# The end of mixer B in a two-layer encoder on one Trainium2 core: row sums through DRAM, and the order and buffers of the last p products

## The chip, the core and the metric

The kernel runs on one core of one Trainium2 chip. TensorE (PE) multiplies and transposes 128x128 blocks into PSUM. VectorE (DVE), ScalarE (ACT) and GpSimd (POOL) do the elementwise work, and SyncE (SP) issues most of the DMAs; its queue is served in order. Each engine runs its own list of instructions in the order in which the program issues them, and waits for the others by semaphores. The metric is the device time of one execution in microseconds; the runs before are given by their median.

## What is computed

The reference is an encoder trunk over 1024 tokens of width 1024, in float32, with two layers. Cut to what matters here:

```python
for i in range(DEPTH):                     # 2 layers
    h = rms_norm(x, norm_g[i])
    if i % 2 == 0:
        y = mixer_a(h, ...)                # neighbourhood attention, 16 heads of 64
    else:
        y = mixer_b(h, ...)                # grouped-query attention, 16 q heads, 4 kv heads
    x = x + y                              # y = (attention * silu(gate)) @ w_out
    g = sigmoid(rms_norm(x, ple_norm_g[i]) @ ple_w_gate[i])
    x = x + g * (p[i] @ ple_w_proj[i])
return rms_norm(x, final_norm_g)
```

Both mixers end their attention with a softmax: the products with v have to be divided by the row sums of the exponentials and multiplied with the gate before the output projection.

## The kernel before

To keep float32 accuracy every matmul is done as three: each operand is split into a high half (`...h`) and a low half (`...l`), and high x high, high x low and low x high are added in PSUM (`split3`, L321). ACT makes the high halves by a copy, DVE the low ones by a subtraction. Weights pass through `wstage` and are split by `WQ.pump` (L215: ACT at L228, DVE at L233), one call of which stands in each pulse.

The program has four stages: mixer A (layer 0), `dense_phase(0)` (output projection in Strassen form, `strassen_out`, and the gated embedding), mixer B (layer 1), `dense_phase(1)`. Each mixer walks through 16 heads, in pairs. In mixer B a step n of 128 is one head, one half `hf` of the tokens and one block of 128 queries t. For each step PE forms scores (`f_S`, L1246, into the pool "s"), DVE their minimum (L1256), ACT the exponential with the row sum in `rs` (`f_E`), PE transposes the result P (`f_T`, L1272, into the pool "t"), ACT and DVE copy it to PTh and PTl (L1274, L1275), and every second step PE multiplies with v (`f_AV`, L1280, into the pool "o", which has one buffer).

The dense products are spread between these pieces by `mix` (L366): a list `att` of attention pieces with costs, a list `dense` of products with costs, and a product is issued as soon as its share of the costs lags behind that of the attention. After each attention piece comes a `pulse` (L345): one `WQ.pump`, and one tick of `post`, a list of closures with a number of ticks to wait. `later` is a second such list; mixer B ticks it once a step, and what is left at the end of a mixer is flushed. In the last quarter of mixer B (g == 3, steps 96 to 127) the dense list holds 16 gate products and the 16 products of p with its projection (`pp_items`), here called p products. A p product is six matmuls into a buffer of the pool "d" (one buffer in mixer B), a copy by ACT to `th` (L629) and a store to DRAM (L630, `ppD`). The last three of the list are held back (`hold`): `mix` issues one of them ahead of the last transposes, where nothing else stands between two sets of transposes (kind "apart"), and two at the very end.

`head_end` (L494) is called by both mixers after the last product with v of a head and a half. ACT copies the lower half of "o" to Y (`evac`, L542), DVE adds the upper half (`join`, L506), which frees "o", and takes the reciprocals of the row sums (`norm`, L532). The sums lie one query to a partition, and are needed one query to a column, in all partitions, in the buffer rb. For pairs 0 to 6 (`rows`, L508) DVE turns a 32x32 block (L510), and SP stores the rows to DRAM (four DMAs, L513) and loads them back spread over the partitions (two DMAs, L515). For pair 7, in both halves, DVE spreads the sums over rb (`spread`, L519), and PE turns them by four transposes (`across`, L525) into PSUM: a buffer of "o" in mixer B, of "t" in mixer A. For the first half ACT copies the result to rb (L528); for the second DVE reads it from PSUM. `DT` holds the ticks after which `across` is issued, five and two. `fin_last` (L554) is the end of pair 7: Y times the gate G (L555), Y times the turned sums (L559), and the high and low halves (L564, L567) into HTh and HTl, which the output projection reads.

The next stage begins with the products of the Strassen form: four blocks with b11, four with b21, four with t2 and so on. Beside the first eight DVE forms the sums S (L1427 to L1435), and it splits the weight t2 (L1401).

Of the kernel before, what the change touches and what calls it, by code (L numbers as in the profile page):

```python
# [11 lines left out]
F32 = mybir.dt.float32  # L12
# [3 lines left out]
AF = mybir.ActivationFunctionType  # L16
# [15 lines left out]
CB = (1.25, 1.0, 2.0, 0.5, 1.0)  # L32
# [2 lines left out]
KT, KN = 2, 4  # L35
DO = (2, 3)
DD = ((3, 2), (3, 2))
DT = (5, 2)
FIN = (4, 4)
HOLD = 2  # L40
ENTRY = 8
# [119 lines left out]
def trunk(ctx, tc, x, wts, rpb, gains, hgains, mask, sides, rope, gain0, out):  # L161
    nc = tc.nc
    sync, act, dve, pool, pe = nc.sync, nc.scalar, nc.vector, nc.gpsimd, nc.tensor
# [152 lines left out]
    post = Later()  # L316
# [28 lines left out]
    def pulse():  # L345
        WQ.pump()
        post.tick()
# [18 lines left out]
    def mix(att, dense, lead=0, hold=0):  # L366
        for f, _ in dense[:lead]:
            f()
            pulse()
        kept = dense[len(dense) - hold:]  # L370
        dense = list(dense[lead:len(dense) - hold])
        total = sum(c for _, c in dense)
        span = sum(c for _, c in att)
        spent = done = 0.0
        since = True
        for i, (f, c) in enumerate(att):
            kind = getattr(f, "kind", None)
            if kind == "apart" and not since and (dense or len(kept) > 2):
                d, e = (dense or kept).pop(0)
                d()  # L380
                spent += e
            if kind in ("apart", "blocks"):
                since = False
            f()
            leave.run()
            pulse()
            done += c
            while dense and spent < total * done / span - 1e-6:
                leave.run()
                leave.wait = i + 1 < len(att) and getattr(att[i + 1][0], "first", False)  # L390
                d, c = dense.pop(0)
                d()
                leave.wait = False
                spent += c
                since = True
        leave.run()
        for f, _ in dense + kept:
            f()
            pulse()
# [94 lines left out]
    def head_end(sb, h, hf, rs, Ops, ylive, layer, gg, talloc):  # L494
        pair = h // 2
        b = (h % 2) * 64
        if h % 2 == 0:
            Y = sb.tile([128, 512], F32, name="Y", bufs=3 if layer == 0 else 2)
            rb = sb.tile([128, 512], F32, name="rb", bufs=2)
            r8 = sb.tile([128, 8], F32, name="r8", bufs=4)  # L500
            ylive[pair, hf] = (Y, rb, r8, {})
        Y, rb, r8, tail = ylive[pair, hf]
        yh = Y[b:b + 64]

        def join():
            dve.scalar_tensor_tensor(yh, Ops[0:64], 0.5, yh, op0=ALU.mult, op1=ALU.add)  # L506

        def rows():  # L508
            r8T = sb.tile([128, 32], F32, name="r8T", bufs=2)
            dve.transpose(r8T.rearrange("p (a c) -> p a c", a=4), r8[:, None].to_broadcast([128, 4, 8]))  # L510
            rD = dram.tile([8, 128], F32, name="rD", bufs=4)
            for b in range(4):
                post.add(DD[layer][1], lambda b=b: sync.dma_start(rD[:, 32 * b:32 * b + 32], r8T[32 * b:32 * b + 8]))  # L513
            for i in range(2):
                post.add(DD[layer][1], lambda i=i: sync.dma_start(  # L515
                    rb[64 * i:64 * i + 64], bass.AP(tensor=rD.tensor, offset=rD.offset + 512 * i, ap=[[0, 64], [1, 512]])))

        def spread():
            dve.tensor_copy(rb.rearrange("p (t j c) -> p t j c", t=4, j=2),  # L519
                            r8.rearrange("p (j t) -> p t j", j=2)[:, :, :, None].to_broadcast([128, 4, 2, 64]))  # L520

        def across():
            ps = talloc()
            for t in range(4):
                pe.transpose(ps[:, t], rb[:, t * 128:(t + 1) * 128], ident)  # L525
            ps = ps.rearrange("p t c -> p (t c)")
            if hf == 0:
                act.activation(rb, ps, AF.Copy)  # L528
            tail["rb"] = rb if hf == 0 else ps

        def norm():
            dve.reciprocal(r8[:, 4 * (h % 2):4 * (h % 2) + 4], rs)  # L532
            if h % 2 == 0:
                return
            if pair < 7:
                post.add(DD[layer][0], rows)
            else:
                spread()
                post.add(DT[hf], across)

        def evac():
            act.activation(yh, Ops[64:128], AF.Copy, scale=0.5)  # L542
            post.add(DY, join)
            norm()
        if h == NH - 1 and hf == 1:
            evac()
        else:
            post.add(DO[layer], evac)
        if h % 2 == 0:
            return None  # L550
        G = gg.pop((pair, hf))
        del ylive[pair, hf]

        def fin_last():  # L554
            dve.tensor_tensor(Y, Y, G, ALU.mult)  # L555
            if "rb" not in tail:
                post.l = [e for e in post.l if e[1] is not across]
                across()
            dve.tensor_tensor(Y, Y, tail["rb"], ALU.mult)  # L559
            y3 = Y.rearrange("p (t c) -> p t c", t=4)  # L560
            ts = slice(4 * hf, 4 * hf + 4)

            def hi():
                act.activation(HTh[:, ts, 7, :], y3, AF.Copy)  # L564

            def lo():
                dve.tensor_tensor(HTl[:, ts, 7, :], y3, HTh[:, ts, 7, :], ALU.subtract)  # L567
            if hf == 0:
                post.add(3, hi)
                post.add(5, lo)  # L570
            else:
                hi()
                lo()

        def fin():
            yhi, ylo = rb.bitcast(F32R), Y.bitcast(F32R)

            def store(c, src):
                sync.dma_start(yD[layer][c][4 * hf:4 * hf + 4, :, pair, :].rearrange("t p c -> p t c"),
                               src.rearrange("p (t c) -> p t c", t=4))  # L580

            def split():
                act.activation(yhi, Y, AF.Copy)
                dve.tensor_tensor(ylo, Y, yhi, ALU.subtract)
                post.add(2, lambda: (store(0, rb), store(1, Y)))
            pool.tensor_tensor(Y, Y, G, ALU.mult)
            pool.tensor_tensor(Y, Y, rb, ALU.mult)
            if pair < 4 and hf == 1:
                post.add(YS[layer] + 2, lambda: store(0, Y))
            else:  # L590
                post.add(YS[layer], split)
        return fin_last if pair == 7 else fin
# [452 lines left out]
    def mixer_b(pend):  # L1045
        with ExitStack() as es:
# [5 lines left out]
            psS = es.enter_context(tc.tile_pool(name="bps", bufs=2, space=PSUM))  # L1052
# [7 lines left out]
            def dalloc():  # L1060
                if pro[0]:
                    pro[1] += 1
                    if pro[1] <= ENTRY:
                        return psS.tile([128, 1024], F32, name="s")[:, :512]
                    if pro[1] % 2 == 0:
                        return psO.tile([128, 512], F32, name="o")
                return pd.tile([128, 512], F32, name="d")

            gg, ylive = {}, {}
            KA, KB, V, QT, QST, P, RS, OP = {}, {}, {}, {}, {}, {}, {}, {}  # L1070
            later = Later()
# [172 lines left out]
            steps = [(2 * p + j, hf, t) for p in range(8) for hf in range(2) for j in range(2) for t in range(4)]  # L1244
# [35 lines left out]
            def f_AV(h, hf, t):  # L1280
                if t == 1:
                    OP[h, hf] = psO.tile([128, 512], F32, name="o")
                o = OP[h, hf][:, (t - 1) * 128:(t + 1) * 128]
                for k in range(NT):
                    mm(o, V[h // 4][:, k], PTh[:, k], t == 1 and k == 0, False)
                while turned:
                    turned.pop(0)()
                for k in range(NT):
                    mm(o, V[h // 4][:, k], PTl[:, k], False, t == 3 and k == NT - 1)
                if t == 3:  # L1290
                    fin = head_end(sb, h, hf, RS[h, hf], OP.pop((h, hf)), ylive, 1, gg, talloc)
                    if fin:
                        later.add(FIN[1], fin)
# [29 lines left out]
            for g in range(4):  # L1323
                att = []
# [26 lines left out]
                    if YLOAD_B <= n < YLOAD_B + NT:  # L1351
                        att.append((lambda t=n - YLOAD_B: load_y(1, t), 0.0))
                if g == 3:
                    att.append((lambda: f_AV(*steps[-1]), CB[1]))
                def gates(p):
                    return [i for hf in range(2) for i in gate_items("bg", p, hf, dalloc, sb, gg)]
                dense = []
# [7 lines left out]
                else:  # L1365
                    WQ.cap[3] = 2
                    dense += gates(2 * g + 1) + pp_items(1, dalloc, sb, TAGS_B)
                mix(att, dense, hold=HOLD + 1 if g == 3 else 0)
            post.flush()
            later.flush()  # L1370
            post.flush()
# [453 lines left out]
```

## Time and profile before

| what | us |
|---|---|
| median of 3 runs | 1514.3 |
| lowest and highest run | 1509.89, 1514.97 |
| the profiled execution | 1510.65 |
| its span, first to last instruction | 1508.9 |
| PE busy | 1483.4 |
| DVE busy | 1088.7 |
| ACT busy | 917.7 |

A row of a timeline in the following reads: start in us from the start of the span, duration in us, engine, line of the kernel, operation, output <- inputs by the program's names, shapes, and a count where several instructions are merged (the duration is then that of them all); in brackets stands how long the engine was idle before it, and what ended that. PE's matmuls are pipelined, so the next one starts before the end that is shown of the last: distances of starts say more than durations. A row of the list of waits reads: engine, what and line that waited, what it waited for, us in total, times, longest. PEld is the load of weights into PE, SPq the DMAs that SP issues.

### The profile page before, as it was taken

The numbers are of one execution on the slowest core, as the hardware profiler recorded it, in microseconds if no ns is written. First come the engines' busy times: TensorE is split into PE (matmuls) and PEld (weight loads), VectorE is DVE, ScalarE is ACT, GpSimd is POOL, SyncE is SP. The second block draws the span as 40 slices with busy tenths as digits, with TensorE's granted clock in tenths as the row PEclk, the third lists the DMA queues.
The fourth block names the chain that finished last, engine by engine and source line by source line (L and its number), as shares of the span: only waits on it lengthen the run. The fifth ranks groups of instructions, "written<-read, shape, count | busy, mean of one in ns | idle before, by whom it ended". The sixth has DMA issues, their size and how long they took to land.

```text
span 1508.9 us, 24794 instructions
## 1 busy us (share of the span) xinstructions
PE 1483.4 (98%) x8885; PEld 1304.4 (86%) x8885; DVE 1088.7 (72%) x2139; ACT 917.7 (61%) x1866; POOL 449.3 (30%) x605
## 2 busy tenths in 40 slices
PE   9999999999999999999999999999999999999997
PEld 8888988988988787888988989989999988888786
DVE  7566476477477498767887786777877887689856
ACT  7676476476477535433567776766767777744432
POOL 1456475386265200010322222443131300000022
PEclk9999999999999999999999999999999999999999
DMA  8334374283132862262210111111111122763123
GB/s 266 123 104 123 79 170 137 64 172 95 36 92 82 324 246 99 91 206 80 76 50 22 33 53 39 43 33 46 55 30 46 39 76 78 230 240 116 56 91 133
DMA packets 91243, 157.45 MB, mean 104 GB/s; under 512 B 18160, under 2 KB 54256, under 8 KB 90608
## 3 DMA queue, kind: packets, MB, share of 16 engines
q1 hardware_dynamic: 85968, 139.86, 28.2%
q0 software_dynamic: 2560, 8.39, 3.7%
q10 hardware_dynamic: 2592, 7.61, 1.5%
q8 instruction: 71, 1.16, 0.3%
q14 instruction: 52, 0.43, 0.1%
HBM read 125.30 MB, written 50.83 MB: 117 GB/s over the span
## 4 chain that ended last, share of the span: by engine, by line
PE 44%; DVE 6%; ACT 2%; issue 1%; POOL 0%; ACTq 0%; DVEq 0%; POOLq 0%
PE d L319 19%; PE o L319 9%; PE s L319 8%; PE t L1272 7%; PE t L319 1%; DVE xn L1607 1%; DVE PTl L1275 1%; DVE X L1503 0%; DVE mn L1256 0%; PE t L1226 0%; DVE HTl L492 0%; DVE HTl L1449 0%; PE t L490 0%; DVE wl L233 0%; DVE th L1665 0%
## 5 line engine op out<-in xcount | busy, mean ns | idle before, releaser
L319 PE MATMUL d<-wh,HTh 128*128 128x256 f32 (+1 forms) x1000 | 332.2, 335 | 0.9 <-DVE X L1503 0.6
L319 PE MATMUL d<-wh,HTl 128*128 128x256 f32 (+1 forms) x1000 | 327.5, 330 | 0.0
L319 PE MATMUL d<-wl,HTh 128*128 128x256 f32 (+1 forms) x1000 | 326.8, 330 | 0.2 <-DVE wl L1401 0.2
L1275 DVE TENSOR_TENSOR PTl<-t,PTh 128x512 fp32r<-128x512 f32 x256 | 164.6, 685 | 106.3 <-ACT PTh L1274 106.0
L319 PEld LDWEIGHTS d<-wh,HTh 128*128 128x128 f32 x1000 | 188.1, 190 | 20.9 <-issue 1.0
L319 PEld LDWEIGHTS d<-wl,HTh 128*128 128x128 f32 x1000 | 188.1, 189 | 19.9 <-DVE wl L1401 0.6
L319 PE MATMUL d<-HTh,wh 128*128 128x512 f32 x504 | 204.7, 406 | 0.0
L319 PEld LDWEIGHTS d<-wh,HTl 128*128 128x128 f32 x1000 | 188.0, 189 | 18.3
L319 PE MATMUL d<-HTh,wl 128*128 128x512 f32 x504 | 198.0, 393 | 0.0
L319 PE MATMUL d<-HTl,wh 128*128 128x512 f32 x504 | 197.4, 392 | 0.0
L1262 ACT ACTIVATE P<-s,mn 128x1024 f32<-128x1024 f32 x128 | 142.9, 1116 | 47.3 <-DVE mn L1256 46.4
L1274 ACT ACTIVATE PTh<-t 128x512 fp32r<-128x512 f32 x256 | 139.4, 595 | 46.0 <-PE t L1272 45.5
L1256 DVE TENSOR_REDUCE mn<-s 128x1 f32<-128x1024 f32 x128 | 155.1, 1211 | 9.8 <-PE s L319 9.3
L798 POOL TENSOR_TENSOR PTh<-PTh,SIDE 128x256 fp32r<-128x256 f32 x96 | 81.2, 846 | 195.4 <-ACT PTh L793 195.4
L1272 PE MATMUL t<-ident,P 128*128 128x128 f32 x1024 | 134.9, 273 | 2.5 <-DVE PTl L1275 2.0
L319 PE MATMUL s<-KA,QS 128*128 128x512 f32 (+2 forms) x384 | 134.2, 403 | 0.3 <-DVE mn L772 0.3
L1272 PEld LDWEIGHTS t<-ident,P 128*128 128x128 f32 x1024 | 115.5, 140 | 12.8 <-DVE PTl L1275 6.9
L319 PE MATMUL s<-KB,QS 128*128 128x512 f32 (+2 forms) x384 | 121.5, 370 | 0.0
L319 PE MATMUL o<-PTl,V 128*128 128x256 f32 (+2 forms) x672 | 120.0, 290 | 1.1 <-DVE PTl L1275 0.6
L319 PE MATMUL o<-PTh,V 128*128 128x256 f32 (+2 forms) x672 | 118.4, 287 | 1.9 <-DVE Y L506 0.8
L233 DVE TENSOR_TENSOR wl<-wstage,wh 128x1024 fp32r<-128x1024 f32 x78 | 98.0, 1258 | 29.8 <-ACT wh L228 29.3
L319 PEld LDWEIGHTS d<-HTh,wl 128*128 128x128 f32 x504 | 94.6, 188 | 21.7
(250 smaller groups left out, 2891.2 us busy)
## 6 DMA issues: line engine op xcount, KB each, us to landing
wstage<-in_wts SPq DMA_DIRECT2D x88, 512.0 KB
pp<-ppD SPq DMA_DIRECT2D x32, 256.0 KB
X<-in_x SPq DMA_DIRECT2D x15, 512.0 KB
rb<-rD SPq DMA_DIRECT2D x56, 128.0 KB
ppD<-th SPq DMA_DIRECT2D x20, 256.0 KB
tD0t<-in_wts SPq DMA_DIRECT2D x16, 256.0 KB
tD1t<-in_wts SPq DMA_DIRECT2D x16, 256.0 KB
xD<-X SPq DMA_DIRECT2D x8, 512.0 KB
```

The lines of the kernel that those rows point to most:

```text
L233: eng.tensor_tensor(lo[:, c:c + n], s[:, c:c + n], hi[:, c:c + n], ALU.subtract)
L319: pe.matmul(ps, a, b, start=first, stop=last, skip_group_check=True)
L798: pool.tensor_tensor(pt[:, 3 * j - 1:3 * j + 4:4], pt[:, f1:f1 + 1].to_broadcast([128, 2, 128]), SIDE[:, :2], ALU.mult)
L1256: dve.tensor_reduce(mn, ps, axis=AX.X, op=ALU.min)
L1262: act.activation(p, ps, AF.Exp, bias=mn, scale=-1.0, accum_out=RS[h, hf][:, t:t + 1])
L1272: pe.transpose(ps[:, i], p[:, k * 128:(k + 1) * 128], ident)
L1274: act.activation(PTh[:, ks, c], ps, AF.Copy)
L1275: dve.tensor_tensor(PTl[:, ks, c], ps, PTh[:, ks, c], ALU.subtract)
L1607: dve.scalar_tensor_tensor(xn, X[t], rn[m][:, i:i + 1], g1, op0=ALU.mult, op1=ALU.mult)
```

## The change

Four edits. In `norm` the first half of pair 7 takes the way of the other pairs: `rows`, through DRAM, with rb ready for `fin_last` by its dependencies alone; the copy out of PSUM in `across` is gone, and `DT` is one number. In `mix` a piece of kind "last" is preceded by a kept product and a pulse. The last products with v in mixer B become such a piece, and four products are kept instead of three, so that one goes ahead of the last transposes, one ahead of the last products with v, and two behind. From that piece on `dalloc` takes turns: the next buffer from the pool "s", the one after from "d".

```diff
-DT = (5, 2)
+DT = 2
...
-            if kind == "apart" and not since and (dense or len(kept) > 2):
+            if kind == "apart" and not since and (dense or len(kept) > 3):
...
+            if kind == "last" and kept:
+                kept.pop(0)[0]()
+                pulse()
             f()
...
-            ps = ps.rearrange("p t c -> p (t c)")
-            if hf == 0:
-                act.activation(rb, ps, AF.Copy)
-            tail["rb"] = rb if hf == 0 else ps
+            tail["rb"] = ps.rearrange("p t c -> p (t c)")
...
-            if pair < 7:
+            if pair < 7 or hf == 0:
                 post.add(DD[layer][0], rows)
+                tail["rb"] = rb
             else:
                 spread()
-                post.add(DT[hf], across)
+                post.add(DT, across)
...
+                if end[0]:
+                    end[0] += 1
+                    if end[0] % 2 == 0:
+                        return psS.tile([128, 1024], F32, name="s")[:, :512]
                 return pd.tile([128, 512], F32, name="d")
...
-                    att.append((lambda: f_AV(*steps[-1]), CB[1]))
+                    def last():
+                        end[0] = 1
+                        f_AV(*steps[-1])
+                    last.kind = "last"
+                    att.append((last, CB[1]))
...
-                mix(att, dense, hold=HOLD + 1 if g == 3 else 0)
+                mix(att, dense, hold=HOLD + 2 if g == 3 else 0)
```

More of the change, by code (lines that the diff above doesn't have):

```diff
@@ L1066, in dalloc @@
                         return psO.tile([128, 512], F32, name="o")
+                if end[0]:
+                    end[0] += 1
+                    if end[0] % 2 == 0:
+                        return psS.tile([128, 1024], F32, name="s")[:, :512]
                 return pd.tile([128, 512], F32, name="d")
+            end = [0]
             gg, ylive = {}, {}
```

## The prediction

> **What bounds the kernel now.** I read the page first, then the list of waits for TensorE over the last quarter of mixer B, then timelines around the two places where rows of sums are turned, then the rows of the DMA queue.
>
> ```profile
> span 1508.9 us, 24794 instructions
> PE   1483.4 (98%) x8885; PEld 1304.4 (86%) x8885; DVE 1088.7 (72%) x2139; ACT 917.7 (61%) x1866; POOL 449.3 (30%) x605
> ```
>
> PE is at 98%: the time is PE's work plus its few waits, so only PE instructions that go and PE waits that go or come count. In the last quarter of mixer B (1184 to 1326 us) the waits are these, with three more in rows below:
>
> ```profile
> PE t L1272 <- DVE PTl L1275: 0.9, 1, 0.9
> PE o L319 <- DVE Y L506: 0.8, 2, 0.5
> ...
> PE o L319 <- ACT PTh L1274: 0.4, 1, 0.4
> ```
>
> There is little to win: some 4 us of waits in 142 us. The diff, however, touches the shared `head_end`, so `pair < 7 or hf == 0` also changes the end of mixer A, which the change's few words leave out. Both ends have to be summed.
>
> **Mixer B, the four transposes that go.** Between the transposes of P and the next scores lie 0.79 us in an ordinary step (1289.17 to 1289.96), and 2.29 us in the step with the transposes of the row sums (1292.36 to 1294.65):
>
> ```profile
> 1289.17 1.04 PE L1272 MATMUL t<-ident,P 128*128 128x128 f32 x8
> ...
> 1289.96 0.71 PE L319 MATMUL s<-KA,QS 128*128 128x512 f32 x2
> ...
> 1292.36 1.03 PE L1272 MATMUL t<-ident,P 128*128 128x128 f32 x8
> ...
> 1294.24 0.66 PE L525 MATMUL o<-ident,rb 128*128 128x128 f32 x4 [0.84 <-DVE Y L506]
> 1294.65 0.71 PE L319 MATMUL s<-KA,QS 128*128 128x512 f32 x2
> ...
> 1306.79 0.69 DVE L559 TENSOR_TENSOR Y<-Y,rb 128x512 f32<-128x512 f32 x1
> ```
>
> The difference, 1.5 us, is the four transposes and their wait for the join of Y, which frees the one o buffer. It goes: **-1.5 us**. ACT also loses the copy of the turned rows. DVE loses a copy and gains a 32x32 transpose, which took 0.20 us for another pair (row below) and lies beside PE's work.
>
> The price is the trip through DRAM: four stores and two loads on SP's queue, the loads waiting there for the stores. Two trips of other pairs bound it, one in a quiet stretch, one among large transfers:
>
> ```profile
> 1263.24 0.20 DVE L510 STREAM_TRANSPOSE r8T<-r 128x32 f32<-128x32 f32 x1
> ...
> 186.98 1.33 SPq L513 DMA_DIRECT2D rD<-r8T  x4
> 192.28 1.09 SPq L515 DMA_DIRECT2D rb<-rD  x2
> ...
> 196.17 1.29 POOL L587 TENSOR_TENSOR Y<-Y,rb 128x512 f32<-128x512 f32 x1 [1.02 <-DMA rb<-rD]
> ...
> 1228.89 1.30 SPq L513 DMA_DIRECT2D rD<-r8T  x4
> 1231.21 1.09 SPq L515 DMA_DIRECT2D rb<-rD  x2
> ...
> 1234.83 1.30 POOL L587 TENSOR_TENSOR Y<-Y,rb 128x512 f32<-128x512 f32 x1 [6.04 <-DMA rb<-rD]
> ```
>
> From the first store to the multiply with rb: 9.2 us loaded (186.98 to 196.17), 5.9 us quiet (1228.89 to 1234.83). In mixer B the stores are issued near 1294.4, once DVE has done the join (the transposes waited for it until 1294.24). Even 9.2 us gives 1303.6. The multiply stood at 1306.79 and moves up by 1.5 to 1305.3, so 1.7 us are left and the trip is hidden: 0. Behind the waiting loads stand on SP a store of a p product and the last loads of y; the store's th buffer is wanted two products later, the y only in the next stage: 0.
>
> **Mixer B, the products placed otherwise.** The planner now spreads 28 instead of 29 products over the same attention costs, so each comes up to one step later, and one of the kept ones goes ahead of the last products with v. Walking the list through: the products with v of steps 111, 113, 123 and 127 get a dense product between themselves and the transposes that they wait for; those of 97, 107, 109 and 117 lose theirs.
>
> ```profile
> 1260.90 1.23 DVE L233 TENSOR_TENSOR wl<-wstage,wh 128x1024 fp32r<-128x1024 f32 x1
> ...
> 1261.02 1.18 PE L319 MATMUL o<-PTh,V 128*128 128x256 f32 x8 [0.32 <-DVE Y L506]
> ...
> 1262.04 1.28 DVE L1275 TENSOR_TENSOR PTl<-t,PTh 128x512 fp32r<-128x512 f32 x2
> ...
> 1262.78 1.33 PE L319 MATMUL o<-PTl,V 128*128 128x256 f32 x8 [0.58 <-DVE PTl L1275]
> ```
>
> Step 113 waited 0.32 + 0.58 = 0.9 us, because a weight's low half sat on DVE ahead of PTl. The gate product that frees that weight's slot moves past the scores, so the low half falls behind PTl, and a dense product stands ahead: **-0.9 us** (bounds 0 and -0.9). The four that lose their product may wait now: 0 to 4 times 0.4 us, the one wait for PTh in the list. Steps 99 and 101, which have no dense product there today, don't appear in the list, so I take a value nearer to zero, **+0.5 us**.
>
> **Mixer B, the last step.**
>
> ```profile
> 1318.89 1.03 PE L1272 MATMUL t<-ident,P 128*128 128x128 f32 x8
> ...
> 1320.27 1.23 PE L319 MATMUL o<-PTh,V 128*128 128x256 f32 x8 [0.35 <-ACT PTh L1274]
> ...
> 1323.86 0.66 PE L525 MATMUL o<-ident,rb 128*128 128x128 f32 x4
> ...
> 1324.86 0.50 PE L319 MATMUL d<-wh,KA 128*128 128x512 f32 x1 [0.34 <-ACT th L629]
> ```
>
> The transposes take 0.79 us, so the products with v could start at 1319.68 instead of 1320.27; the p product ahead covers that 0.6, less some 0.1 for its own wait for the one d buffer: **-0.5 us**. After the four transposes of the second half (1323.86, 0.41 us as at 1294.24) PE could go on at 1324.27; it waits for the copy out of d until 1324.86. With a second pool it doesn't: **-0.6 us**. Mixer B in sum: -1.5 - 0.9 + 0.5 - 0.5 - 0.6 = **-3.0 us**. The low bound adds the other 0.5 us of the list's line for the join of Y, with no new wait: -1.5 - 0.9 - 0.6 - 0.6 - 0.5 = -4.1. The high one keeps the wait of step 113 and takes all four new ones: -1.5 + 1.6 - 0.5 - 0.6 = -1.0.
>
> That carries into the output projection, where DVE has room: its low half of t2 starts at 1343.97, 2.35 us for two, and PE first wants it at 1348.33.
>
> ```profile
> 1343.97 2.35 DVE L1401 TENSOR_TENSOR wl<-wstage,wh 128x1024 fp32r<-128x1024 f32 x2
> ...
> 1348.33 0.39 PE L319 MATMUL d<-wl,HTh 128*128 128x512 f32 x1
> ```
>
> **Mixer A.** Here the same trip comes at a bad time.
>
> ```profile
> 517.38 0.32 SPq L630 DMA_DIRECT2D ppD<-QS  x1
> ...
> 519.74 0.50 PE L319 MATMUL d<-wh,HTh 128*128 128x512 f32 x1 [0.30 <-ACT G L629]
> ...
> 521.15 0.69 DVE L559 TENSOR_TENSOR Y<-Y,rb 128x512 f32<-128x512 f32 x1 [2.90 <-ACT rb L528]
> ...
> 540.96 2.36 DVE L1401 TENSOR_TENSOR wl<-wstage,wh 128x1024 fp32r<-128x1024 f32 x2
> ...
> 542.23 0.50 PE L319 MATMUL d<-wl,HTh 128*128 128x512 f32 x1 [0.19 <-DVE wl L1401]
> ```
> ```profile
> 516.00:522.00 6.00, 5.24 (x27) 3.89 (x26) 3.01 (x7) 2.63 (x4) 0.00 (x0) 1.00 1.05 407
> 522.00:525.00 3.00, 3.00 (x15) 2.49 (x14) 2.20 (x4) 1.73 (x3) 0.00 (x0) 1.00 0.15 55
> 525.00:542.00 17.00, 17.00 (x76) 13.77 (x74) 16.59 (x24) 6.23 (x10) 0.00 (x0) 1.00 0.81 307
> ```
>
> (columns: stretch, length, busy PE, PEld, DVE, ACT, POOL, clock, DMA share, GB/s.) Counting pulses, the stores are issued behind the last p product, that is behind the store at 517.38 on SP: from 517.7. The DMA engines are full (1.05) until 522 and nearly idle after (0.15). The first leg so lasts until some 522.2, as the loaded one took 5.3 us (186.98 to 192.28) and the quiet one 2.3; the second leg, in quiet, takes 3.6 us (1231.21 to 1234.83): rb is there at 525.8. DVE multiplies at 521.15 now, so it stands 4.7 us longer, with everything of the next stage queued behind it on DVE: the second half's multiply, both low halves, two weights, the sums S. From 525 to 542 DVE is busy 16.59 of 17 us, with no room to catch up, and at 542.23 PE is already waiting for the end of that chain. PE's start at 519.74 doesn't move up for the four transposes that go, since it waits for the copy out of d. So the whole delay lands on PE: **+4.7 us**; by the quiet trip 517.7 + 5.9 = 523.6, +2.5; by the loaded one 526.9, +5.7.
>
> The Trainium skill, "DMA: Bandwidth & Descriptors", section Queues, rings and completion order, says that each DMA engine takes the descriptors of a ring in order; the longer first leg of the loaded trip agrees. The same page, section Anatomy of one DMA, puts a fixed 2.0 us on each DMA; an estimate from it alone, two legs after 1.3 and 1.1 us of issue, would be 517.7 + 6.4 = 524.1, +3.0 here and 0.0 in all. The rows under load speak against it.
>
> **Sum.** +4.7 - 3.0 = **+1.7 us**. The profiled execution took 1510.65 us (span 1508.9, 1.75 around it): 1512.4. It lies 3.65 below the median of the three runs, 1514.3; carried to the median, which is what is compared: **1516.0 us**.
>
> **Rivals.**
> First, the delay in mixer A doesn't reach PE, or only the 2.5 us of the quiet trip, because DVE has slack after all. For it: PE's own wait there is only 0.19 us. Against it: DVE's 16.59 of 17 us. Then -3.0 to -0.5 us remain, 1511.3 to 1513.8; faster by over 0.3% only if mixer B gives its bound of -4.1 and the scatter of the runs helps.
> Second, slower: the trip in mixer A is longer than both that are shown. Place: SP's queue at 517.7, where the stores of rb's sums, then the loads, then the last p store follow one another behind a full DMA. Price: each us that rb is late is a us of PE. Against the -3.0 it decides from a delay of 7.5 us, rb at 528.7, a trip of 11 us; the loaded trip took 9.2. For it: stretch 525 to 542 has the DMA at 0.81 again, so a first leg that slips past 525 meets the next stage's loads. Then +4.5 to +6: 1518.8 to 1520.3.
> Third, the change does less than it says in mixer B: PE comes 1.5 us earlier and then waits for PTh and PTl, since ACT and DVE have the same work in the same order; of -3.0 only the last step's -1.1 is left, in all +3.6: 1517.9.
>
> **Chances.** Forecast 0.57, first rival 0.18, second 0.12, third 0.13. About 0.3%, 4.5 us, is what a measurement of this kernel can tell from no change: its own runs reach from 1509.89 to 1514.97. The second rival counts as slower, a third of the first (0.06) as faster, the rest as same, less 0.07 for scatter to either side: faster 0.13, same 0.68, slower 0.19. The range takes the sum's bounds, 2.5 - 4.1 = -1.6 and 5.7 - 1.0 = +4.7 (1512.7 to 1519.0); below it a median that falls to the lower runs, 4.4 under 1512.7 (1508); above it most of the second rival (1520).
>
> **What would show it.** Right: no transposes of rb at 1294 and the next scores 0.8 us after the transposes of P; no PE wait before the last d; in mixer A, DVE's multiply with rb waiting for the DMA rb<-rD until near 526, and PE waiting some 5 us for the low half of t2 near 546. Wrong: PE going through 520 to 550 without that wait, or a wait for rb near 1305 in mixer B.

## The result and the profile after

The changed kernel takes 1519.97 us (median of 6 runs, 1517.84 to 1523.03), the kernel before 1514.13 us (6 runs, 1509.89 to 1515.25). The medians differ by 5.8 us; the ratio of the compared runs is 1.0052, 95% interval 1.0041 to 1.0062, which is 7.9 us (6.2 to 9.4): **slower by some 0.5%**. The profiled execution took 1518.3 us. Its page begins:

```profile
span 1516.5 us, 24790 instructions
...
PE 1486.0 (98%) x8877; PEld 1304.1 (86%) x8877; DVE 1087.5 (72%) x2139; ACT 917.1 (60%) x1864; POOL 448.2 (30%) x605
```

The span is 7.6 us longer, although PE has eight matmuls less. The list of PE's waits around the end of mixer A and through the dense stage (500 to 700 us) names the largest part:

```profile
PE d L319 <- DVE wl L1411: 4.6, 1, 4.6
PE t L319 <- DVE wl L233: 1.6, 1, 1.6
PE d L319 <- ACT G L630: 0.7, 1, 0.7
PE t L528 <- DVE r8T L513: 0.5, 1, 0.5
```

(Line numbers differ by a few from kernel to kernel, as lines were added or taken away.) Before, PE waited 0.19 us for the low half of t2; now 4.6 us, and 1.6 us for another low half ahead of it. The timeline of the changed kernel follows it back (L516 and L518 are the stores and loads of the trip, L560 the multiply with rb, L1411 the low half of t2):

```profile
518.36 2.43 SPq L516 DMA_DIRECT2D rD<-r8T  x4
...
520.00 0.50 PE L319 MATMUL d<-wh,HTh 128*128 128x512 f32 x1 [0.74 <-ACT G L630]
...
524.21 1.09 SPq L518 DMA_DIRECT2D rb<-rD  x2
...
527.75 0.69 DVE L560 TENSOR_TENSOR Y<-Y,rb 128x512 f32<-128x512 f32 x1 [9.12 <-DMA rb<-rD]
...
547.56 2.35 DVE L1411 TENSOR_TENSOR wl<-wstage,wh 128x1024 fp32r<-128x1024 f32 x2
...
548.83 0.80 PE L319 MATMUL d<-wl,HTh 128*128 128x512 f32 x1 [4.58 <-DVE wl L1411]
```

Times of different executions are compared from a common point: the first product of the output projection (519.74 before, 520.00 after). DVE multiplies with rb 1.41 us behind it before and 7.75 us after; PE starts on the low half of t2 22.49 us behind it before and 28.83 us after. Both differences are 6.3 us.

In mixer B the four transposes at the end of step 121 are gone, and PE waits elsewhere. Its waits from 1190 to 1345 us in the changed kernel:

```profile
PE t L1278 <- DVE PTl L1281: 2.2, 4, 0.9
PE t L1278 <- ACT th L1234: 0.5, 1, 0.5
PE o L319 <- ACT PTh L1280: 0.2, 1, 0.2
PE o L319 <- DVE Y L509: 0.2, 1, 0.2
```

Of the first line, 0.9 us belong to step 103 and stood in the kernel before too. Such a list shows only when PE stood still. What a step costs is seen better in the distance between the starts of two sets of transposes, less 1.36 us (six matmuls) for each d product between them. Here are steps 113 to 117 in the kernel before, and the same in the changed one:

```profile
1258.74 1.03 PE L1272 MATMUL t<-ident,P 128*128 128x128 f32 x8
...
1265.33 1.03 PE L1272 MATMUL t<-ident,P 128*128 128x128 f32 x8
...
1268.50 1.03 PE L1272 MATMUL t<-ident,P 128*128 128x128 f32 x8
...
1272.65 1.03 PE L1272 MATMUL t<-ident,P 128*128 128x128 f32 x8
...
1275.83 1.03 PE L1272 MATMUL t<-ident,P 128*128 128x128 f32 x8
```
```profile
1265.82 1.03 PE L1278 MATMUL t<-ident,P 128*128 128x128 f32 x8
...
1270.92 1.03 PE L1278 MATMUL t<-ident,P 128*128 128x128 f32 x8
...
1271.46 1.18 DVE L1262 TENSOR_REDUCE mn<-s 128x1 f32<-128x1024 f32 x1
...
1272.67 1.12 ACT L1268 ACTIVATE P<-s,mn 128x1024 f32<-128x1024 f32 x1 [1.89 <-DVE mn L1262]
...
1273.78 1.08 ACT L1280 ACTIVATE PTh<-t 128x512 fp32r<-128x512 f32 x2
...
1274.40 1.29 DVE L1281 TENSOR_TENSOR PTl<-t,PTh 128x512 fp32r<-128x512 f32 x2 [1.76 <-ACT PTh L1280]
...
1275.15 1.25 PE L1278 MATMUL t<-ident,P 128*128 128x128 f32 x8 [0.88 <-DVE PTl L1281]
...
1275.61 1.09 SPq L518 DMA_DIRECT2D rb<-rD  x2
...
1276.80 7.10 SPq L631 DMA_DIRECT2D ppD<-th  x3
...
1280.91 0.60 PE L1278 MATMUL t<-ident,P 128*128 128x128 f32 x4
...
1281.37 0.60 ACT L1234 ACTIVATE th<-t 128x512 f32<-128x512 f32 x1 [3.17 <-DMA ppD<-th]
...
1282.02 0.66 PE L1278 MATMUL t<-ident,P 128*128 128x128 f32 x4 [0.51 <-ACT th L1234]
...
1285.10 1.04 PE L1278 MATMUL t<-ident,P 128*128 128x128 f32 x8
```

In the three stretches that follow one d product stands in both kernels, so they compare as they are. From the transposes of step 113 to those of 114 it was 6.59 us and is 5.10: the forecast wait is gone, and more. But 114 to 115 was 3.17 and is 4.23: a weight's low half (L233, 1270.20 to 1271.41 on DVE) stands ahead of the minimum of the next scores, ACT's exponential waits for the minimum, and the copy PTh of step 114 stands behind the exponential; PTl comes later still, and the transposes of step 115 wait for the buffers that it frees. From 116 to 117 it was 3.18 and is 4.19. There `q_stack` (a helper that turns the q of a later pair, once in eight steps, through the pool "t") copies its result into a "th" buffer at L1234. It waits for the store of a p product, and that store stands on SP's queue behind the loads of rb of pair 6 (1275.61).

Added up for the last quarter of mixer B, from the transposes of step 95 to the last matmul of the last p product (142.90 us before, 143.14 after):

| part | forecast | measured |
|---|---|---|
| step 121, transposes of the sums | -1.5 | -1.74 |
| step 113, its two waits | -0.9 | -1.49 |
| the four steps that lose their product | +0.5 | +1.15 |
| the other steps, 96 to 125 | 0 | +3.97 |
| last steps and end | -1.1 | -1.65 |
| sum | -3.0 | +0.24 |

### The profile page after: what moved, and what is told of

Read it like the earlier page. It is cut to its first block, busy times and chain, and to the rows that moved or that the text cites. A ratio compares the mean times of both kernels' runs of the same rounds, so it can differ in the third digit from the quotient of the medians.

```text
span 1516.5 us, 24790 instructions
## 1 busy us (share of the span) xinstructions
PE 1486.0 (98%) x8877; PEld 1304.1 (86%) x8877; DVE 1087.5 (72%) x2139; ACT 917.1 (60%) x1864; POOL 448.2 (30%) x605
## 3 DMA queue, kind: packets, MB, share of 16 engines
q8 instruction: 70, 1.15, 0.3%
## 4 chain that ended last, share of the span: by engine, by line
PE 42%; DVE 6%; ACT 2%; issue 2%; DMA 0%; POOL 0%; ACTq 0%; DVEq 0%; POOLq 0%
PE d L319 18%; PE s L319 8%; PE o L319 8%; PE t L1278 7%; DVE PTl L1281 1%; PE t L319 1%; DVE xn L1617 1%; DVE mn L1262 1%; ACT PTh L1280 0%; DVE X L1513 0%; PE t L1232 0%; DVE HTl L495 0%; ACT P L1268 0%; DVE HTl L1459 0%; DVE wl L233 0%
## 5 line engine op out<-in xcount | busy, mean ns | idle before, releaser
L233 DVE TENSOR_TENSOR wl<-wstage,wh 128x1024 fp32r<-128x1024 f32 x78 | 98.0, 1258 | 33.7 <-ACT wh L228 33.5
```

The lines of the kernel that those rows point to most:

```text
L233: eng.tensor_tensor(lo[:, c:c + n], s[:, c:c + n], hi[:, c:c + n], ALU.subtract)
```

## The experiments

Times are against the kernel before on the same chip in each case (median 1510.8 to 1511.2 us there), with the 95% interval in us worked out from that of the ratio. "Quarter" is the stretch of the table above, in the profiled execution. In the first kernel below, whose mixer B is that of the kernel before, the quarter takes 142.64 us instead of 142.90: two executions of the same program for this stage can differ by 0.26 us, and differences of that size say nothing.

**One layer at a time.** In the kernel before, `norm` sends the first half of pair 7 through DRAM in mixer A alone:

```diff
-            if pair < 7:
+            if pair < 7 or (hf == 0 and layer == 0):
                 post.add(DD[layer][0], rows)
+                if pair == 7:
+                    tail["rb"] = rb
```

> The kernel before with one edit: in mixer A alone the reciprocal row sums of the last pair's first half go through DRAM. Theory A (the time comes from mixer A: the round trip ends 6.6 us later than the four broadcasting transposes did, and PE waits that much longer at the low half of t2): about +6.6 us, 1520.7. Rival B (PE makes up mixer A's later start by work it finds elsewhere, and the +5.8 us of the changed kernel sit in mixer B's new order): between 0 and +1 us.

Measured: 1517.83 us, ratio 1.0047 (1.0033 to 1.0061), +7.1 us (+5.0 to +9.2). The timeline has the same chain as the changed kernel:

```profile
516.57 2.43 SPq L513 DMA_DIRECT2D rD<-r8T  x4
...
518.23 0.50 PE L319 MATMUL d<-wh,HTh 128*128 128x512 f32 x1 [0.74 <-ACT G L631]
...
522.45 1.09 SPq L515 DMA_DIRECT2D rb<-rD  x2
...
526.00 0.69 DVE L561 TENSOR_TENSOR Y<-Y,rb 128x512 f32<-128x512 f32 x1 [9.13 <-DMA rb<-rD]
...
547.07 0.74 PE L319 MATMUL d<-wl,HTh 128*128 128x512 f32 x1 [4.58 <-DVE wl L1403]
```

547.07 - 518.23 = 28.84 us, as in the changed kernel. Theory A holds; rival B falls: mixer A alone costs all that the change costs.

The same edit with `layer == 1`:

> The kernel before with one edit: in mixer B alone the row sums of the last pair's first half go through DRAM; the order of the d products stays as it was. Theory A (the order's waits, not the trip, eat mixer B's gain): the wait of step 113 and the transposes of step 121 go, the trip is hidden, -1.5 to -3 us, 1511.1 to 1512.6. Rival B (the trip's DMAs on SP hold back the stores of the p products and so make the waits themselves): 0 to +2 us.

Measured: 1509.65 us, 0.9994 (0.9984 to 1.0003), -0.9 us (-2.4 to +0.5). The quarter takes 141.36 us, -1.54. The stretch of step 121 moved (-1.44); the end moved by no more than executions differ (-0.27). The trip is hidden, and its DMAs make no wait by themselves. Step 113 keeps its 6.60 us: that wait belongs to the order of the products, not to the way of the sums. So theory A was right about the trip and wrong to count step 113's wait here, and the timing alone, whose interval holds zero, would not settle it; the trace does.

**The order alone.** The kernel before with the two edits of the change to `mix`, the piece "last" and `hold=HOLD + 2`:

> The kernel before with one edit: one kept product more and a p product ahead of the last products with v, so that the planner places the d products of mixer B's last stretch otherwise; row sums as before, pools as before. Theory A (the new placement's waits on exponentials, weights' low halves and p buffers cost about 4.6 us, the last step gives 0.4 to 1.1 back): +2.5 to +4 us. Theory A', that the placement costs only beside the DMAs of the trip: -1 to 0 us. Rival B of the run on mixer A (all in mixer B) asks for +5 us or more.

Measured: 1512.44 us, 1.0005 (0.9996 to 1.0014), +0.8 us (-0.6 to +2.1); quarter 144.30 us, +1.40. (One of its eleven executions took 8397.53 us, for a reason that no trace shows; the ratio is without it.) The four steps that lose their product cost +1.13, the other steps +2.98, step 113 gives 1.48 back, the last steps and the end 1.31; the 0.08 that are left lie in step 121. Below theory A's bound, but a cost where the forecast had a gain of 0.9 (-0.9 + 0.5 - 0.5), and without any trip of the last pair through DRAM. The waits are those of the changed kernel, except that the transposes of the sums, still there in step 121, wait for the join of Y:

```profile
PE t L1275 <- DVE PTl L1278: 2.2, 4, 0.9
PE o L528 <- DVE Y L509: 1.2, 1, 1.2
PE o L319 <- ACT PTh L1277: 0.2, 1, 0.2
PE o L319 <- DVE Y L509: 0.2, 1, 0.2
```

**The changed kernel without mixer A's part**: `norm` and `across` of the change, but with layer 0 on the transposes (`if pair < 7 or (hf == 0 and layer == 1)`, the copy to rb and `DT = (5, 2)` back).

> The changed kernel with mixer A's last pair put back on the four broadcasting transposes; mixer B as changed. Theory A: 6.6 us less than the changed kernel, about 1513.4, which is -0.7 against the kernel before. Rival B (the cost is mixer B's): +5 us or more against the kernel before, 1519.

Measured: 1509.55 us, 0.9992 (0.998 to 1.0003), -1.2 us (-3.0 to +0.5); quarter 142.27 us, -0.63. PE's start on the low half of t2 is back at 22.49 us behind the first product of the projection. Mixer B's three parts add up: -1.54 for the sums, +1.40 for the order and -0.57 for the pools (next run) make -0.71, and -0.63 was measured. In the changed kernel the same program for this stage took 0.9 us more, 0.7 of it from step 116 to 117, at the wait behind `q_stack`. That wait depends on when DMAs land, and so differs between executions.

**The pools alone**: the kernel before with the alternating `dalloc` of the change.

> The kernel before with one edit: from the last products with v of mixer B on, d products take turns between the pools s and d. Theory A: the wait of the last d product for the copy out of d (0.34 us, and 0.6 between the transposes and it) goes, -0.4 to -0.6 us, all of it in the last 10 us of the stage. Rival: the wait moves to the join of Y ahead of the four transposes, 0 us.

Measured: 1510.19 us, 0.9997 (0.9987 to 1.0006), -0.5 us (-2.0 to +0.9); quarter 142.33 us, -0.57, all of it behind the last transposes of P. As forecast in the trace; too small for the timing.

**The placement as before, the rest as changed.** The kernel above (mixer A on the transposes), with the fourth kept product counted in the planner's total:

```diff
-        total = sum(c for _, c in dense)
+        total = sum(c for _, c in dense) + sum(c for _, c in kept[:max(0, hold - HOLD - 1)])
```

> The changed kernel with mixer A's last pair put back on the transposes, and with the fourth kept product counted in the planner's total, so that the d products of steps 96 to 125 stand where the kernel before had them; the product ahead of the last products with v and the second pool stay. Theory A (the changed placement costs 4.0 us of PE time in steps 97 to 120 and saves 1.5 at step 113): 2.5 us less than the same kernel with the changed placement, -3 us against the kernel before, no wait of the transposes for PTl beyond the one of 0.9 us. Rival (the waits come from the trip's DMAs or from the p product ahead of the end, not from the placement): as the kernel with the changed placement, -1 us against the kernel before.

Measured: 1509.4 us, 0.9989 (0.998 to 0.9998), -1.7 us (-3.0 to -0.3); quarter 141.28 us, -1.62. Against the kernel with the changed placement the steps that lost their product win 1.15 and the others 2.63, step 113 loses 1.50, steps 121 to 122 0.29, and the end 1.00: no product is left for step 126, and the transposes of step 127 wait 0.34 us for PTl. Net -0.99 of the expected -2.5. Direction and place are as theory A has them; steps 121 and 122 and the end were not in its sum.

**Where the first leg goes in mixer A.** Four kernels like the first one of this section. In the first, the 32x32 block is turned at once after the reciprocals and its DMAs follow one pulse later:

```diff
+            at = DD[layer][1] if pair < 7 else 1
...
-                post.add(DD[layer][0], rows)
+                post.add(DD[layer][0], rows) if pair < 7 else rows()
```

> The kernel before with mixer A's row sums through DRAM, but the 32x32 block turned at once after the reciprocals and its DMAs issued one pulse later, so that the four stores stand on SP's queue some 3 to 4 us earlier, ahead of the last loads of HTh and HTl. Theory A1 (a store waits for what was put on the queue's ring ahead of it): the first leg ends 2 to 4 us earlier, PE's wait for the low half of t2 shrinks from 4.6 us to 1 to 2.5, +2.5 to +4.5 us. Theory A2 (the first leg ends only when the DMA engines run empty, near 522, wherever the stores stand): the wait stays at 4 us or more, +6 us.

Measured: 1516.83 us, 1.0039 (1.0023 to 1.0054), +5.9 us (+3.5 to +8.2). The stores were issued 2.65 us ahead of the first product of the projection, in the changed kernel 1.64, and rb was multiplied 6.79 us behind it, there 7.75. They stood on SP behind a p store that waited for its copy, so they gained one us, not three or four.

In the second the stores are issued with no pulse in between:

```diff
+            def put(f):
+                f() if pair == 7 else post.add(DD[layer][1], f)
             for b in range(4):
-                post.add(DD[layer][1], lambda b=b: sync.dma_start(
+                put(lambda b=b: sync.dma_start(
```

> The kernel before with mixer A's row sums through DRAM, the four stores issued at the very point of the reciprocals, with no pulse between, so that they stand on SP's queue ahead of the last two to four loads of HTh and HTl. Theory A1 (a store waits for the bytes put on its ring ahead of it, and then some 2 us): the first leg ends 1 to 3 us before the DMA engines run empty, PE's waits in mixer A shrink by 2 to 5 us, +1.5 to +4 us. Theory A2 (stores and loads share full engines until they run empty, wherever the stores stand): the first leg ends 2 us behind the end of the loads as before, +5.5 to +6.5 us.

Measured: 1515.76 us, 1.003 (1.0018 to 1.0041), +4.5 us (+2.7 to +6.2). Issued 2.93 us ahead, multiplied 6.48 us behind. The interval of the time reaches into both expectations; the first leg, 5.84 us as in the changed kernel (5.85), is that of theory A2. The loads of HTh and HTl still stood ahead of the stores on SP. The stores overtook one p store of 256 KB in the first of the two kernels and two in the second (by the 411 GB/s in the rows below, an estimate of 0.6 us each), and rb won 1.0 and 1.3 us.

The other two take the stores off SP's queue, to ACT's and to POOL's:

```diff
-                post.add(DD[layer][1], lambda b=b: sync.dma_start(rD[...
+                post.add(DD[layer][1], lambda b=b: (act if pair == 7 else sync).dma_start(rD[...
```

> The kernel before with mixer A's row sums through DRAM, the four stores issued from ACT's queue instead of SP's. Theory A1 (the stores wait behind what stands on SP's ring): on another ring the first leg takes 2 to 3.5 us instead of 5.9, rb comes 2.5 to 4 us earlier, +2.5 to +4.5 us. Theory A2 (the DMA engines are full for every ring until near 522): the first leg takes 5 us or more, +6 us. A cost of its own on ACT: four issues ahead of the last copies out of d, up to +1 us.

> The kernel before with mixer A's row sums through DRAM, the four stores issued by POOL, whose queue holds no loads of HTh and HTl. Theory A1 (the wait is for the ring): the first leg ends well before the DMA engines run empty, some 3 us after its issue, +2 to +4 us. Theory A2 (full engines hold up every ring): it ends some 2 us after the engines run empty, +6 us. A cost of its own: POOL prepares its descriptors itself, up to 1 us for each store.

Measured: ACT 1517.78 us, 1.0043 (1.0029 to 1.0057), +6.5 us (+4.4 to +8.6); POOL 1517.25 us, 1.0041 (1.0027 to 1.0055), +6.2 us (+4.1 to +8.3). No gain on either. (ACT issued them only 0.6 us ahead of the first product, behind a copy.) On POOL the trip and the DMA engines (stretch, length, busy PE, PEld, DVE, ACT, POOL, clock, DMA share, GB/s) look like this:

```profile
516.48 2.05 POOL L513 DMA_DIRECT2D rD<-r8T  x4 [4.27 <-DVE r8T L510]
...
523.40 1.09 SPq L515 DMA_DIRECT2D rb<-rD  x2
...
526.90 0.69 DVE L561 TENSOR_TENSOR Y<-Y,rb 128x512 f32<-128x512 f32 x1 [9.30 <-DMA rb<-rD]
```
```profile
518.00:520.00 2.00, 1.26 (x6) 0.87 (x6) 0.00 (x0) 1.54 (x2) 0.54 (x2) 1.00 1.05 411
520.00:522.00 2.00, 2.00 (x10) 1.68 (x9) 0.00 (x0) 0.00 (x0) 0.00 (x0) 1.00 0.79 281
522.00:524.00 2.00, 2.00 (x10) 1.66 (x9) 0.00 (x0) 0.00 (x0) 0.00 (x0) 1.00 0.02 5
```

The stores were issued from 516.48, the engines carried next to nothing from 522, and still SP could issue the loads only at 523.40. In all six kernels with this trip, from SP, ACT and POOL, the loads are issued 1.2 to 2.4 us behind the first quarter of a us in which less than half of the DMA engines' time is busy. The trace also holds the single packets that the DMA engines moved. The four stores are 32 packets of 128 bytes, the only ones of that size there:

| kernel | first store issued | first packet starts, last one ends | loads issued |
|---|---|---|---|
| changed | 518.36 | 521.93, 523.02 | 524.21 |
| ACT's queue | 517.91 | 520.57, 522.09 | 523.43 |
| POOL's queue | 516.48 | 520.32, 522.41 | 523.40 |
| before, the quiet trip | 1228.89 | 1229.66, 1230.73 | 1231.21 |

In the six kernels the first packet starts 2.7 to 3.8 us behind the first issue, against 0.8 us in the quiet trip, and the last one ends 1.0 to 1.3 us ahead of the loads. Theory A1 falls: on no queue did the stores pass the transfers that ran; their packets came only as the engines emptied. The first leg was the time until the engines were through with what was issued before, and then some 2 us. (What would have been if the loads of HTh and HTl came later was not tried.)

The same five kernels and the changed one show what a late rb costs. Multiply with rb, and start on t2, in us behind the first product of the projection:

| kernel | multiply | t2 |
|---|---|---|
| before | 1.41 | 22.49 |
| stores at once | 6.48 | 27.56 |
| stores a pulse later | 6.79 | 27.86 |
| mixer A alone, changed kernel | 7.77, 7.75 | 28.84, 28.83 |
| POOL's queue | 7.93 | 29.01 |
| ACT's queue | 8.64 | 29.72 |

In every row t2 starts 21.07 to 21.08 us behind the multiply: each us of rb is a us of PE.

**Step 113.** To the placement as before, one swap: no product from the planner behind the products with v of step 111 until the scores of step 114 are issued, and none ahead of the transposes of step 113.

```diff
-            if kind == "apart" and not since and (dense or len(kept) > 3):
+            if kind == "apart" and not since and not (hold > HOLD and i == 80) and (dense or len(kept) > 3):
...
-            while dense and spent < total * done / span - 1e-6:
+            while dense and spent < total * done / span - 1e-6 and not (hold > HOLD and 75 <= i <= 77):
```

> The kernel of the earlier placement (mixer A on the transposes, row sums of mixer B through DRAM, placement of steps 96 to 125 as before, a p product ahead of the last products with v, two pools) with one swap more: the gate product of step 112 moves behind the scores of step 114, and the p product of step 113 moves behind its transposes, ahead of the products with v. Theory A (the 1.5 us of step 113 are its two waits, for the join of Y and for PTl behind a weight's low half): the stretch from the transposes of step 113 to those of 114 falls from 6.6 to 5.1 us, nothing else moves, -4 us against the kernel before. Rival (the low half of the weight only moves on and holds up the transposes of step 115, as in the changed kernel): the 1.5 us reappear as 1 us at step 115, -2.5 to -3 us.

Measured: 1510.68 us, 0.9999 (0.999 to 1.0008), -0.2 us (-1.5 to +1.2); quarter 140.78 us, -2.12. The step gives back 1.36 us, and step 115 has no wait. But from the transposes of step 116 to those of 117 it is 4.32 us, 1.14 more than before:

```profile
1269.58 1.09 SPq L518 DMA_DIRECT2D rb<-rD  x2
...
1270.78 11.96 SPq L634 DMA_DIRECT2D ppD<-th  x4
...
1274.64 0.60 ACT L1237 ACTIVATE th<-t 128x512 f32<-128x512 f32 x1 [2.08 <-DMA ppD<-th]
...
1275.29 0.66 PE L1281 MATMUL t<-ident,P 128*128 128x128 f32 x4 [0.90 <-ACT th L1237]
```

So in the trace the rival's size (1 us that comes back) was near and its mechanism wrong: not the low half, but the th buffer behind a store behind the loads of rb, the wait of the changed kernel again. The time, -0.2 us, fits neither expectation, and its interval doesn't reach the quarter's -2.12. In the profiled execution the first product of mixer A's projection stands at 522.08 us instead of 519.74, ahead of all that the edit touches; whether the other executions lose their time there too is not shown.

**A buffer of its own for `q_stack`**, on top of that swap:

```diff
-                raw = sb.tile([128, 512], F32, name="th")
+                raw = sb.tile([128, 512], F32, name="qr", bufs=1)
```

> The kernel with the swap at step 113 and, as one edit more, a buffer of its own for the copy of the turned q (raw in q_stack), which until now took turns with the p products in the two th buffers. Theory A (the copy waits for a p product's store, which stands on SP's queue behind the loads of rb; in the kernel with the swap alone this ate 1.1 of the 1.4 us of the swap): the wait of the transposes for ACT's copy near 1275 (0.9 us) goes, the interval to the transposes of step 117 falls from 4.3 to 3.2 us, 1.1 us less than the kernel with the swap, -3 to -3.5 us against the kernel before. Rival (the next wait in line, for PTl or for the store itself, takes its place): no change, -1 to -2 us.

Measured: 1507.88 us, 0.9979 (0.9969 to 0.9988), -3.2 us (-4.7 to -1.8): faster than both kernels. The quarter takes 139.65 us, -3.25; steps 116 to 117 are back at 3.18 us. What is left of PE's waits from 1185 to 1340 us:

```profile
PE t L1281 <- DVE PTl L1284: 1.3, 2, 0.9
PE o L319 <- DVE Y L509: 0.5, 1, 0.5
```

Theory A holds: the chain from SP's queue over the th buffer to the transposes was worth 1.1 us.

## Why the prediction was wrong

**The bound, and mixer A's part: right.** That the diff reaches into mixer A, that PE's start would not move, and that DVE has no room between the multiply and t2, so that the whole delay lands on PE: all shown, the last in six kernels to within 0.02 us. The first rival (no delay on PE) is refuted.

The forecast sum was +1.7 us; the two places where the change acts give +6.5 in the traces. Of the 4.8 us between them mixer A's term has 1.6 and mixer B's 3.2. The median of 1519.97 lies at the very end of the range, which the prediction had stretched to 1520 for its second rival and not for what happened.

**The size of mixer A's term was off.** "+4.7 us" was 6.3 in the trace. The step that failed is "The first leg so lasts until some 522.2": I ended it where the DMA engines run empty. They did so near 522.3, but the loads were issued at 524.21. The first leg took 5.85 us instead of 4.5; counted from the first product of the projection, the stores were issued 0.4 us later than forecast, and the second leg took 3.54 us against 3.6. The DMA share of the changed kernel falls from 1.03 to 0.18 while the loads still wait (columns as in the prediction):

```profile
520.00:522.00 2.00, 2.00 (x9) 1.66 (x10) 0.00 (x0) 0.89 (x1) 0.00 (x0) 1.00 1.03 389
522.00:524.00 2.00, 2.00 (x11) 1.65 (x10) 0.00 (x0) 0.00 (x0) 0.00 (x0) 1.00 0.18 61
```

The Trainium skill, "DMA: Bandwidth & Descriptors", section Anatomy of one DMA, says of DMAs that GpSimd issues that most of a fixed 2 us is the receipt of the last write; here, on SP's, ACT's and POOL's queues, the loads were issued 1.0 to 1.3 us behind the end of the stores' last packet, and 1.2 to 2.4 us behind the full stretch. The prediction weighed the same 2 us as an alternative to the queue, where they belong behind it. The same page, section Queues, rings and completion order, says that a DMA's semaphore write lands only after every earlier write of that DMA engine, across its queues; by the packets this can explain at most those last 1.0 to 1.3 us, since on ACT's and POOL's queues too the packets themselves came late, and no run here isolates why they did. The trip took 9.4 us, not the 11 of the second rival, whose slip of the stores into the next stage's loads did not occur; its price, a us of PE for each us of rb, is the one that the runs show.

**Mixer B's gain failed, at the step "+0.5 us".** The terms for the transposes (-1.5, measured -1.74), step 113 (-0.9, measured -1.49) and the end (-1.1, measured -1.65) were all on the safe side. But the new placement cost 5.1 us instead of 0.5. I counted only the products with v that lose the dense product ahead of them; these four came to +1.15, inside my bounds. The other 3.97 us lie in steps where it is the transposes themselves that wait, one step later, for the t buffers which PTl and `q_stack`'s copy free; for these I had no term and no bound. Two mechanisms make up 2.1 of them. One is the low half of a weight ahead of the minimum (step 115, +1.06): it is read from the rows and gone with the old placement, but no run removes it alone. The other is the th buffer held by a p store behind waiting loads on SP (step 117, +1.0, where the next d product waits as well): it is shown, as a buffer of its own takes away the 1.1 us that it cost in the kernel with the swap. The prediction did name what stands on SP behind the loads of the trip, "the store's th buffer is wanted two products later", and put it at 0, but looked at the trip of pair 7 only, and not at who else uses th. The smaller waits at steps 111, 112, 116, 119, 120, 123 and 124 (0.2 to 0.4 each) were not taken apart one by one.

The third rival (the gain of mixer B not realised) had the right sign and a related reason, but kept the last step's 1.1 as a gain; in all, +6.3 from mixer A and +0.2 from mixer B make 6.5 of the 7.6 us between the spans. The other 1.1 lie in stretches that the change doesn't touch, and single executions differ by that much: the last quarter of mixer B begins at 1182.28 us in the kernel with the pools alone, and at 1183.22 in the kernel before, which are alike up to there.

## What to carry to other kernels

A round trip through DRAM issued while the DMA engines were full had its first leg end only some 2 us after they had run empty, and its second leg, in quiet, took another 3.5 us: look at the DMA share at the point of issue, and see whether what waits for the trip has slack. When a planner is given another number of items, each step of its whole stretch is a changed step: walk through all the resources that turn over there (here the buffers of "t" and "th"), not only through the pieces that lose a neighbour. And when a shared function is edited for one stage, price it in every stage that calls it.

## What the runs showed of the hardware

Issuing four stores of 1 KB from another engine's queue did not bring them past the large transfers that ran: 5.5 us on ACT's queue and 6.9 us on POOL's until the loads that wait for them were issued, against 5.8 to 5.9 on SP's; their packets began 2.7 us behind the first issue on ACT's queue, 3.8 on POOL's and 3.3 to 3.7 on SP's. The four issues on SP took 2.43 us in the changed kernel beside a DMA share of 1.05, and 1.30 us in a quiet stretch; but they took 1.29 us at 1263.47 in the kernel before, where the share was 0.98 for that short time, so what stretches them is not shown.
